# Two blocks of the first expert matrix, and two units of the query weights, joined into one 8 KB piece per partition

## The chip, the cores and the metric

One core of a Trainium2 chip runs the program. The metric is the device time of one execution in microseconds (us), the median of three runs. The engines are PE (TensorE), DVE (VectorE), ACT (ScalarE), POOL (GpSimd) and SP (SyncE); transfers go over the core's 16 DMA engines, which the queues of SP, ACT and POOL share.

## What is computed

Two layers over 256 tokens of width 1024. Each layer has a mixer (attention, a short convolution, gates, projections) and then the PEER block, around which the change lies. Its core, cut from the reference:

```python
q = (hf @ w_query).reshape(T, PEER_HEADS, 2, PEER_HALF)
scores = jnp.einsum("thpd,hpnd->thpn", q, sub_keys)
...
expert_idx = jnp.take_along_axis(cand_i, best_pos, axis=-1)
gates = jax.nn.softmax(best_v, axis=-1)
...
u = jnp.take(expert_u, xc["idx"], axis=0)
vv = jnp.take(expert_v, xc["idx"], axis=0)
a = jax.nn.gelu(jnp.einsum("td,thkd->thk", xc["h"], u))
return jnp.einsum("thk,thkd->td", xc["g"] * a, vv)
```

Each token picks 16 of 16384 experts in each of 8 heads. All matrices are float32; `expert_u` ("U", the first expert matrix) and `expert_v` ("V") have 64 MB each per layer, `w_query` 8 MB.

## The kernel before

**Two ways for two halves of the tokens.** The first 128 tokens are done densely: PE multiplies them by all of U (128 units of 128 experts, `experts`, L1099), a gelu and one-hot weights select what counts (L1071 to L1088), and PE multiplies by all of V (L1157). The other 128 tokens are done by gathers: 256 indirect DMAs per layer, issued by POOL (L991), each bringing one expert row of 4 KB for each of the 128 tokens, half of them from the rows of U and half from the rows of V. DVE takes up each gather: `use` (L1002) multiplies a U row by the token's vector and sums it (L1007), or adds a weighted V row into `y1` (L1015).

**Gathers.** There are eight buffers of 512 KB for them (`NROWS`). `use` hands its buffer back and `issue` (L985) starts the next gather into it, so a gather's time from issue to use cannot be longer than the time in which DVE takes up eight. While the U units run, one `use` stands behind each unit, and beside it a portion of the routing (`route_all`, L1026: top-k and index arithmetic on DVE), until the routing is done. All of this order is fixed when the program is built. `factors` (L897) ends the routing: it turns the selections by PE transposes that DVE copies out, in between its other work.

**The stream of weights.** Everything that is read densely goes through one list, `stream`, in groups of 1 MB: two units of 512 KB in a tile of 128 partitions by 2 by 1024 floats. `pairs` (L79) makes a group of two units that lie one behind the other in memory: the tile's partition then holds 4 KB of one unit and 4 KB of the next. `load_ahead` (L175) walks the list and starts a transfer on SP's queue (L198) whenever a place is free: three `raw` tiles, and, for the query weights and U alone, "spare" places (`spare_part`, L157): parts of the buffers `ah` and `al` that will hold the results later, `hot`, and the gather buffers `rows` before the first gather. So SP has up to 16 places as the query weights end, fewer and fewer during the U stage, and 3 at its end. `dense_done` (L356) gives a place back when PE has issued its matmuls, and SP's transfer waits for these.

For V the two units of a group are neighbours in a row of memory (unit `j` of row `i` is row 128`i`+`j`), so that a partition's 8 KB are one piece already. Ahead of a V group, SP waits for a mark that DVE sets in its own order (`marks`, L195); a U or query group has no such mark. The query weights and U are laid out by `lay_out` on the host (L1220), unit by unit:

```python
"w_query": blocks(np.asarray(i["w_query"]), 16),
"expert_u": np.asarray(i["expert_u"]).reshape(L, 128, 128, KD, 128)
            .transpose(0, 2, 4, 3, 1).reshape(L, 128, 128, D),
```

Of the kernel before, what the change touches and what calls it, by code (L numbers as in the profile page):

```python
# [17 lines left out]
DEPTH, S, D = 2, 256, 1024  # L18
NT = S // 128
KD = D // 128  # L20
# [5 lines left out]
NE = 128  # L26
# [20 lines left out]
def body(ctx: ExitStack, tc: tile.TileContext, d: dict, out: bass.AP):  # L47
    nc = tc.nc
    V, A, G, T = nc.vector, nc.scalar, nc.gpsimd, nc.tensor
# [27 lines left out]
    groups = []  # L77

    def pairs(kind, ap, n):  # L79
        for u in range(0, n, 2):  # L80
            groups.append((kind, [(slice(0, 2), ap[u:u + 2].rearrange("u p c -> p u c"))]))

    def ada_pair(l, r, m):

        a = d["w_adat"]
        return (("col", l, r, m), [(slice(0, 1), a[l, r, m]), (slice(1, 2), a[l, r + 1, m])])

    def ada_rows(l, r, k):
        a = d["w_adag"][l, r].rearrange("(k p) c -> k p c", p=128)
        return (("row", l, r, k), [(slice(0, 2), a[k:k + 2].rearrange("u p c -> p u c"))])  # L90

    def weave(main, extra, first=0):

        extra = deque(extra)
        res, n, m = [], len(extra), len(main) - first
        for i, g in enumerate(main):
            res.append(g)
            while extra and (n - len(extra)) * m < (i + 1 - first) * n:
                res.append(extra.popleft())
        assert not extra  # L100
        return res

    def take_groups():
        g = list(groups)
        groups.clear()
        return g

    stream = []
    for l in range(DEPTH):
        n = NFIRST[l]  # L110
        pairs("qk", d["w_qk"][l, :n], n)
        pairs("v", d["w_v"][l], 4)
        pairs("qk", d["w_qk"][l, n:], 8 - n)
        pairs("conv", d["w_cv"][l], 12)
        pairs("gate", d["w_gt"][l], 16)
        for u in range(4):
            groups.append(("proj", [(slice(0, 1), d["w_ap"][l][u:u + 1].rearrange("u p c -> p u c")),
                                    (slice(1, 2), d["w_cp"][l][u:u + 1].rearrange("u p c -> p u c"))]))
        a = take_groups()
        ex = [ada_rows(l, r, k) for r in range(2) for k in range(0, KD, 2)]  # L120
        if l == 0:
            cols = [ada_pair(0, 0, m) for m in range(KD)]
            parts = {"c": cols, "u": a[:n // 2], "v": a[n // 2:n // 2 + 2]}
            a = a[n // 2 + 2:]
            start = [parts[ch].pop(0) for ch in START]
            assert not any(parts.values())
            ex = [ada_pair(0, 2, m) for m in range(KD)] + ex
        else:
            ex = [ada_pair(l, 2, m) for m in range(KD)] + ex
        pairs("out", d["w_out"][l].rearrange("(k p) c -> k p c", p=128), 8)  # L130
        a += take_groups()
        if l + 1 < DEPTH:
            ex += [ada_pair(l + 1, 0, m) for m in range(KD)]
        if l == 0:
            a = start + weave(a, ex)
        else:
            a = weave(a, ex, 4)
        stream += a
        pairs("query", d["w_query"][l], 16)
        stream += take_groups()  # L140
        u_ap = d["expert_u"][l]
        v_ap = d["expert_v"][l].rearrange("(i j) c -> j i c", j=128)
        for kind, src in (("U", u_ap), ("V", v_ap)):
            for u in range(0, NE, 2):
                groups.append((kind, [(slice(0, 2), src[u:u + 2].rearrange("u p c -> p u c"))]))
        stream += take_groups()

    state = {"dma": 0, "unit": 0, "out": 0, "out0": 0, "v": 0}
# [1040 lines left out]
    for l in range(DEPTH):  # L1189
# [20 lines left out]
        pairs = [xp.tile([128, 2, D], F32, name=f"rows{i}") for i in range(NROWS // 2)]  # L1210
# [9 lines left out]
def lay_out(i):  # L1220
    import numpy as np

    def c(a):
        return np.ascontiguousarray(a)

    L = DEPTH
    w = np.asarray(i["w_in"])
    ada = np.asarray(i["w_ada"]).reshape(L, D, 6, D)
    ab = np.asarray(i["b_ada"]).reshape(L, 6, D)

    def blocks(a, n):
        return a.reshape(L, KD, 128, n, 128).transpose(0, 3, 2, 1, 4).reshape(L, n, 128, D)

    def proj(a):
        a = np.asarray(a).reshape(L, 4, 128, 4, 2, 128).transpose(0, 3, 2, 4, 1, 5)
        return a.reshape(L, 4, 128, D)

    r = {
        "x": np.asarray(i["x"]).reshape(S, D),
        "c": np.asarray(i["c"]),  # L1240
        "c_col": np.asarray(i["c"]).reshape(KD, 128).T,
        "norm_g": np.stack([np.asarray(i["norm1_g"]), np.asarray(i["norm2_g"])], 1).reshape(L, 2, KD, 128).transpose(3, 0, 1, 2),
        "w_adat": ada[:, :, [0, 1, 3, 4]].reshape(L, D, 4, KD, 128).transpose(0, 2, 3, 4, 1),
        "w_adag": ada[:, :, [2, 5]].transpose(0, 2, 1, 3),
        "b_ada": ab[:, [0, 1, 3, 4]].reshape(L, 4, KD, 128).transpose(3, 0, 1, 2),
        "b_gate": ab[:, [2, 5]],
        "w_qk": blocks(w[:, :, :1024], 8).reshape(L, 2, 4, 128, D).transpose(0, 2, 1, 3, 4).reshape(L, 8, 128, D),
        "w_v": w[:, :, 1024:1536].reshape(L, 4, 2, 128, 512).transpose(0, 1, 3, 2, 4).reshape(L, 4, 128, D),
        "w_cv": w[:, :, 1536:3072].reshape(L, KD, 128, 3, 4, 128).transpose(0, 4, 3, 2, 1, 5).reshape(L, 12, 128, D),
        "w_gt": blocks(w[:, :, 3072:], 16),  # L1250
        "conv_w": np.asarray(i["conv_w"]).reshape(L, 3, 4, 128).transpose(3, 0, 2, 1),
        "w_ap": proj(i["w_attn_proj"]),
        "w_cp": proj(i["w_conv_proj"]),
        "w_out": np.asarray(i["w_out"]),
        "w_query": blocks(np.asarray(i["w_query"]), 16),
        "sub_keys": np.asarray(i["sub_keys"]).reshape(L, 16, 128, 128).transpose(0, 3, 1, 2),
        "expert_u": np.asarray(i["expert_u"]).reshape(L, 128, 128, KD, 128).transpose(0, 2, 4, 3, 1).reshape(L, 128, 128, D),
        "expert_v": np.asarray(i["expert_v"]),
        "expert_rows": np.asarray(i["expert_u"]),
        "final_g": np.asarray(i["final_g"]).reshape(1, D),  # L1260
    }
    return {k: c(a) for k, a in r.items()}


def build(arrays):
    import concourse.bacc as bacc

    nc = bacc.Bacc("TRN2", target_bir_lowering=False, num_devices=1)
    d = {}
    for k, a in arrays.items():  # L1270
        d[k] = nc.dram_tensor(f"in_{k}_dram", a.shape, mybir.dt.from_np(a.dtype), kind="ExternalInput").ap()
    o = nc.dram_tensor("out_0_dram", (S, D), F32, kind="ExternalOutput").ap()
    with tile.TileContext(nc) as tc:
        body(tc, d, o)
    return nc
# [9 lines left out]
```

## Time and profile before

| | before |
|---|---|
| time, median of 3 runs | 1833.51 us (1832.49 to 1835.61) |
| the profiled execution | 1834.56 us, its span 1832.8 us |
| PE busy | 1600.5 us (87%) |
| DVE busy | 1390.8 us (76%) |
| POOL, ACT busy | 634.9 us (35%), 577.5 us (32%) |
| moved by DMA | 669.22 MB, mean 365 GB/s |
| chain that ended last | DMA 33%, DVE 31%, PE 26% |

The table is from the profile's page. Shares of busy time are averages over the stages: in each layer the mixer, then the query weights, then U (about 273 to 612 us in the first layer, 1170 to 1505 us in the second), then V. "Chain" is followed back from the last instruction, at each step to what released it.

### The profile page before, as it was taken

Reading aid. Unit: us, or ns where it says so; the run is one execution under the profiler, and the core shown is the slowest. Engines: PE = TensorE matmul, PEld = TensorE weight load, DVE = VectorE, ACT = ScalarE, POOL = GpSimd, SP = SyncE. Lnnn points to the kernel's source line nnn. Section 1 sums busy time; section 2 is a strip of 40 time slices with the busy share of each in tenths; the row PEclk is TensorE's granted clock in tenths of the full one; section 3 lists DMA queues with packets and bytes.
Section 4 is the critical chain, followed back from the end, with each engine's and each line's share of the span. In section 5 each row is a group of like instructions: output and inputs, shape, how many; then the busy total and the mean of one; then the engine's idle time right before and its main releaser. Section 6 shows DMA issues by size and latency. Waiting matters only on the chain.

```text
span 1832.8 us, 26002 instructions
## 1 busy us (share of the span) xinstructions
PE 1600.5 (87%) x9527; PEld 1257.6 (69%) x9527; DVE 1390.8 (76%) x2872; ACT 577.5 (32%) x1257; POOL 634.9 (35%) x540
## 2 busy tenths in 40 slices
PE   6899999968599988977789999997886999888776
PEld 5789779967599645522268997897886994444222
DVE  7798859999888777745467875899997887676455
ACT  3464322111166334200047434221113653331001
POOL 1000004444544555555400000244444445334551
PEclk8899999988899999999999999998898999999999
DMA  8769779999999999999955877899999999999996
GB/s 334 263 228 357 294 312 357 408 408 407 409 368 405 414 414 416 415 415 415 397 218 192 293 278 297 321 391 408 409 404 397 388 403 415 414 415 415 416 414 277
DMA packets 163201, 669.22 MB, mean 365 GB/s; under 512 B 16001, under 2 KB 16001, under 8 KB 146690
## 3 DMA queue, kind: packets, MB, share of 16 engines
q1 hardware_dynamic: 87346, 396.39, 55.1%
q0 software_dynamic: 73856, 268.48, 37.0%
q10 hardware_dynamic: 1872, 2.69, 0.4%
q8 instruction: 75, 1.23, 0.3%
q14 instruction: 52, 0.43, 0.1%
HBM read 666.46 MB, written 1.05 MB: 364 GB/s over the span
## 4 chain that ended last, share of the span: by engine, by line
DMA 33%; DVE 31%; PE 26%; issue 5%; ACT 3%; POOL 1%; SPq 0%; POOLq 0%; DVEq 0%; ACTq 0%
DMA rows<-in_expert_v_dram,idx 20%; DVE rows L1007 8%; PE mm L1099 8%; DMA rows<-in_expert_rows_dram,idx 5%; DMA raw<-in_expert_v_dram 5%; PE yp L1157 4%; PE wp L1086 3%; DVE y L1015 3%; PE mm L394 3%; DVE wl L345 2%; PE mm L395 2%; PE mm L396 2%; DVE raw L288 2%; ACT wh L340 1%; DVE ti L838 1%
## 5 line engine op out<-in xcount | busy, mean ns | idle before, releaser
L991 POOL DMA_INDIRECT rows<-in_expert_rows_dram,idx x256 | 292.2, 1142 | 783.3 <-PE mm L940 239.8
L1015 DVE SCALAR_TENSOR_TENSOR y<-rows,cv,y 128x1024 f32<-128x1024 f32 x254 | 325.7, 1282 | 161.2 <-DMA rows<-in_expert_v_dram,idx 156.4
L991 POOL DMA_INDIRECT rows<-in_expert_v_dram,idx x256 | 327.0, 1277 | 294.4 <-DMA rows<-in_expert_v_dram,idx 105.0
L1007 DVE SCALAR_TENSOR_TENSOR rows<-rows,h 128x1024 f32<-128x1024 f32 x256 | 307.5, 1217 | 19.4 <-DMA rows<-in_expert_rows_dram,idx 19.0
L1157 PE MATMUL yp<-raw,ah 128*128 128x512 f32 x512 | 240.8, 617 | 65.8 <-DMA raw<-in_expert_v_dram 64.6
L1157 PE MATMUL yp<-raw,al 128*128 128x512 f32 x512 | 239.3, 611 | 31.2 <-DMA raw<-in_expert_v_dram 30.3
L1099 PE MATMUL mm<-hfull,raw 128*128 128x128 f32 x1984 | 239.7, 280 | 19.6 <-ACT al L1113 16.8
L1099 PEld LDWEIGHTS mm<-hfull,raw 128*128 128x128 f32 x1984 | 231.1, 195 | 20.4 <-ACT al L1113 17.2
L1071 ACT ACTIVATE hot<-iotf,iT 128x128 f32<-128x128 f32 x512 | 163.4, 390 | 257.8 <-PE wp L1086 212.4
L1157 PEld LDWEIGHTS yp<-raw,ah 128*128 128x128 f32 x512 | 95.3, 194 | 209.8 <-DMA raw<-in_expert_v_dram 108.2
L1099 PE MATMUL mm<-hfull,ah 128*128 128x128 f32 x1600 | 195.1, 284 | 13.3 <-ACT al L1113 13.3
L1099 PEld LDWEIGHTS mm<-hfull,ah 128*128 128x128 f32 x1600 | 191.6, 201 | 13.6 <-ACT al L1113 13.6
L1157 PEld LDWEIGHTS yp<-raw,al 128*128 128x128 f32 x512 | 93.2, 192 | 134.2 <-issue 94.9
L345 DVE TENSOR_TENSOR wl<-raw,wh 128x1024 fp32r<-128x1024 f32 x112 | 135.0, 1222 | 41.4 <-ACT wh L340 40.4
L394 PE MATMUL mm<-hh,wh 128*128 128x256 f32 x512 | 148.5, 290 | 3.8 <-ACT qT L658 3.3
L1086 PEld LDWEIGHTS wp<-hot 128*128 128x128 f32 x1024 | 128.9, 192 | 28.7 <-issue 28.7
L395 PE MATMUL mm<-hl,wh 128*128 128x256 f32 x512 | 145.8, 285 | 0.0
L396 PE MATMUL mm<-hh,wl 128*128 128x256 f32 x512 | 145.7, 285 | 0.0
L340 ACT ACTIVATE wh<-raw 128x1024 fp32r<-128x1024 f32 x112 | 115.8, 1052 | 70.7 <-DMA raw<-in_w_gt_dram 26.6
L1086 PE MATMUL wp<-hot 128*128 128x64 f32 x1024 | 127.8, 268 | 0.0
L394 PEld LDWEIGHTS mm<-hh,wh 128*128 128x128 f32 x512 | 99.2, 194 | 9.9 <-issue 4.0
L395 PEld LDWEIGHTS mm<-hl,wh 128*128 128x128 f32 x512 | 99.2, 194 | 0.0
(228 smaller groups left out, 2112.4 us busy)
## 6 DMA issues: line engine op xcount, KB each, us to landing
raw<-in_expert_v_dram SPq DMA_DIRECT2D x128, 1024.0 KB
raw<-in_expert_u_dram SPq DMA_DIRECT2D x62, 1024.0 KB
ah<-in_expert_u_dram SPq DMA_DIRECT2D x50, 1024.0 KB
raw<-in_w_adat_dram SPq DMA_DIRECT2D x64, 512.0 KB
raw<-in_w_gt_dram SPq DMA_DIRECT2D x16, 1024.0 KB
raw<-in_w_adag_dram SPq DMA_DIRECT2D x16, 1024.0 KB
raw<-in_w_cv_dram SPq DMA_DIRECT2D x12, 1024.0 KB
raw<-in_w_qk_dram SPq DMA_DIRECT2D x8, 1024.0 KB
```

Source lines behind the costliest of these rows:

```text
L340: A.activation(h, raw, AF.Copy)
L345: l_engine().tensor_tensor(lo, raw, f(h), op=OP.subtract)
L394: T.matmul(ps, h[:, c], mh[:, k], start=first, stop=False)
L395: T.matmul(ps, h[:, c], ml[:, k], start=False, stop=False)
L396: T.matmul(ps, lo[:, c], mh[:, k], start=False, stop=last)
L991: G.indirect_dma_start(out=t, out_offset=None, in_=rows[kind], in_offset=bass.IndirectOffsetOnAxis(ap=idx[:, s:s + 1], axis=0))
L1007: V.scalar_tensor_tensor(t, t, 1.0, h1, op0=OP.mult, op1=OP.mult, accum_out=av[:, s:s + 1])
L1015: V.scalar_tensor_tensor(y1, t, cv[:, s:s + 1], y1, op0=OP.mult, op1=OP.add)
L1071: A.activation(p[:, i], iotf, AF.Abs, bias=iT[:, b * TB + i:b * TB + i + 1])
L1086: T.matmul(ps[:, t], p[:, t], q[:, t], start=True, stop=True)
L1099: T.matmul(ps[:, u + x], raw[:, x, k * 128:(k + 1) * 128], hf[:, k, :128], start=(k == 0), stop=(k == KD - 1))
L1157: T.matmul(ys[q], halves[i // 64][:, i % 64], raw[:, x, q * 512:(q + 1) * 512], start=(i == 0), stop=(i == NE - 1))
```

## The change

The host lays two units side by side: for each partition first the 4 KB of the one, then the 4 KB of the other. A new helper `joined` makes one group of each such double unit, so that a partition's 8 KB are one piece in memory. It replaces `pairs` for the query weights (8 groups per layer) and for U (64 groups per layer). V keeps `pairs`, and everything else is as it was: the same 1 MB into the same tiles in the same order.

```diff
+    def joined(kind, ap):
+        for u in range(ap.shape[0]):
+            groups.append((kind, [(slice(0, 2), ap[u])]))
...
-        pairs("query", d["w_query"][l], 16)
+        joined("query", d["w_query"][l])
         stream += take_groups()
-        u_ap = d["expert_u"][l]
-        v_ap = d["expert_v"][l].rearrange("(i j) c -> j i c", j=128)
-        for kind, src in (("U", u_ap), ("V", v_ap)):
-            for u in range(0, NE, 2):
-                groups.append((kind, [(slice(0, 2), src[u:u + 2].rearrange("u p c -> p u c"))]))
+        joined("U", d["expert_u"][l])
+        pairs("V", d["expert_v"][l].rearrange("(i j) c -> j i c", j=128), NE)
         stream += take_groups()
...
+    def two(a):
+        return a.reshape(L, -1, 2, 128, D).transpose(0, 1, 3, 2, 4)
...
-        "w_query": blocks(np.asarray(i["w_query"]), 16),
+        "w_query": two(blocks(np.asarray(i["w_query"]), 16)),
...
-        "expert_u": np.asarray(i["expert_u"]).reshape(L, 128, 128, KD, 128).transpose(0, 2, 4, 3, 1).reshape(L, 128, 128, D),
+        "expert_u": two(np.asarray(i["expert_u"]).reshape(L, 128, 128, KD, 128).transpose(0, 2, 4, 3, 1).reshape(L, 128, 128, D)),
```

SP's transfers at the change from query weights to U in the first layer, before (a name such as `al<-in_expert_u_dram` is place and source, then partitions by pieces by floats):

```order
L198 DMA raw<-in_w_query_dram 128x2x1024 x3
L198 DMA rows_2296<-in_w_query_dram 128x2x1024
L198 DMA al<-in_w_query_dram 128x2x1024 x4
L198 DMA hot<-in_expert_u_dram 128x2x1024
L198 DMA ah<-in_expert_u_dram 128x2x1024 x4
```

The same place in the changed kernel, where L199 is the line that was L198:

```order
L199 DMA raw<-in_w_query_dram 128x2048 x3
L199 DMA rows_2296<-in_w_query_dram 128x2048
L199 DMA al<-in_w_query_dram 128x2048 x4
L199 DMA hot<-in_expert_u_dram 128x2048
L199 DMA ah<-in_expert_u_dram 128x2048 x4
```

Nothing has moved; two pieces of 1024 floats have become one of 2048. The other engines' instructions are the same in the same order. V's transfers have that form before the change already:

```order
L198 DMA raw<-in_expert_v_dram 128x2048 x3
L196 DMA marks<-in_c_dram 1x1
L198 DMA raw<-in_expert_v_dram 128x2048
```

These are SP's first transfers of V in the first layer; the marks stand only there.

## Rows read from the trace of the kernel before

**Rows 1.** Busy time by stretch: us, PE PEld DVE ACT POOL busy (count), clock, DMA share, GB/s

```profile
273.00:487.00 214.00, 187.10 (x1506) 182.70 (x1504) 205.87 (x581) 37.95 (x62) 103.17 (x90) 0.94 1.00 394
487.00:504.00 17.00, 0.17 (x1) 0.17 (x2) 10.90 (x12) 0.19 (x1) 9.80 (x9) 0.57 1.03 410
504.00:612.00 108.00, 108.00 (x943) 108.00 (x944) 88.40 (x173) 65.73 (x171) 49.40 (x44) 0.97 1.00 391
...
1383.00:1398.00 15.00, 0.00 (x0) 0.00 (x0) 9.95 (x9) 0.00 (x0) 8.61 (x8) 0.63 1.03 410
```

**Rows 2.** The same view, saturated stretches of the U and the V stage

```profile
340.00:440.00 100.00, 80.73 (x682) 80.16 (x681) 96.19 (x280) 13.67 (x19) 46.28 (x40) 0.91 1.03 409
...
700.00:900.00 200.00, 164.86 (x463) 76.45 (x463) 117.37 (x194) 29.55 (x75) 110.69 (x83) 0.99 1.02 415
```

**Rows 3.** What DVE waited for, first layer's query and U stage: total us, times, longest

```profile
DVE y L1015 <- DMA rows<-in_expert_v_dram,idx: 6.0, 5, 1.5
...
DVE rows L1007 <- DMA rows<-in_expert_rows_dram,idx: 0.3, 1, 0.3
```

**Rows 4.** The same for the second layer

```profile
DVE y L1015 <- DMA rows<-in_expert_v_dram,idx: 5.0, 5, 1.4
```

**Rows 5.** Groups of DVE's instructions, 300 to 440 us: count, busy, mean ns, idle before

```profile
L1007 DVE SCALAR_TENSOR_TENSOR rows<-rows,h 128x1024 f32<-128x1024 f32 x57 | 68.3, 1214 | 0.3 <-DMA rows<-in_expert_rows_dram,idx 0.3
```

**Rows 6.** The page's DMA packets, and its queues (q1 is SP's, q0 the gathers')

```profile
DMA packets 163201, 669.22 MB, mean 365 GB/s; under 512 B 16001, under 2 KB 16001, under 8 KB 146690
...
q1 hardware_dynamic: 87346, 396.39, 55.1%
```

**Rows 7.** DMA queues (packets, MB, share), U stage, 380 to 400 us

```profile
q0 software_dynamic: 1125, 4.10, 51.6%
q1 hardware_dynamic: 1054, 4.06, 50.8%
```

**Rows 8.** DMA queues, V stage, 852 to 855 us

```profile
q1 hardware_dynamic: 112, 0.92, 73.7%
q0 software_dynamic: 104, 0.37, 30.7%
```

**Rows 9.** SP's timeline in the U stage: start, us, instruction, count

```profile
341.15 0.37 SPq L198 DMA_DIRECT2D al<-in_expert_u_dram  x1
...
348.29 11.09 SPq L198 DMA_DIRECT2D ah<-in_expert_u_dram  x4
362.59 7.51 SPq L198 DMA_DIRECT2D raw<-in_expert_u_dram  x3
388.19 0.37 SPq L198 DMA_DIRECT2D hot<-in_expert_u_dram  x1
391.76 11.09 SPq L198 DMA_DIRECT2D ah<-in_expert_u_dram  x4
```

**Rows 10.** DMA queues and issues, 287 to 373 us

```profile
q1 hardware_dynamic: 4400, 16.99, 50.4%
...
ah<-in_expert_u_dram SPq DMA_DIRECT2D x8, 1024.0 KB
raw<-in_expert_u_dram SPq DMA_DIRECT2D x6, 1024.0 KB
al<-in_expert_u_dram SPq DMA_DIRECT2D x4, 1024.0 KB
hot<-in_expert_u_dram SPq DMA_DIRECT2D x2, 1024.0 KB
```

**Rows 11.** The chain that ended last, 405 to 440 us: start, us, what

```profile
415.52 17.47 DMA rows<-in_expert_rows_dram,idx
```

**Rows 12.** DVE's timeline, 478 to 506 us: start, us, instruction [idle before]

```profile
495.66 1.28 DVE L1015 SCALAR_TENSOR_TENSOR y<-rows,cv,y 128x1024 f32<-128x1024 f32 x1 [1.44 <-DMA rows<-in_expert_v_dram,idx]
498.22 1.28 DVE L1015 SCALAR_TENSOR_TENSOR y<-rows,cv,y 128x1024 f32<-128x1024 f32 x1 [1.28 <-DMA rows<-in_expert_v_dram,idx]
```

**Rows 13.** What PE waited for, 230 to 612 us

```profile
PE wp L901 <- DVE iT L905: 17.1, 1, 17.1
```

## The prediction

> **What bounds the kernel now.** I read the stages first, then who waits in them, then the DMA queues. The change touches only SP's transfers of the query weights and of U, so what counts is what ends last while those are in flight. In the windows [rows 1] the reader should see a U stage of three parts. From 273 to 487 us DVE is busy 205.87 of 214 us: routing and gathers on DVE set the pace, and PE, which could go faster, is tied to it. From 487 to 504 us PE stands still (0.17 us busy) until DVE has copied `iT` out [rows 13], and DVE on its side takes up V gathers as they land. From 504 to 612 us PE is busy all the time. The second layer repeats this; its standstill is from 1383 to 1398 us [rows 1].
>
> The DMA engines are full long before anything waits for them: 409 GB/s with a share of 1.03 from 340 to 440 us [rows 2], where DVE nevertheless waits 0.3 us in all for gathers of U rows [rows 3]. In that stretch DMA is fully used and yet not what ends last. How close it is: the gather issued at 415.52 us took 17.47 us and stands on the chain [rows 11]. DVE takes up 57 gathers in 140 us [rows 5], one per 2.46 us, so eight buffers are one round of 19.7 us; less 1.2 us of use and about 1 us of POOL, some 17.5 us is all that a gather may take. The gathers have **no lead left at 415 us**.
>
> **What the change does to each transfer.** Nothing is added, removed or moved: 64 U and 8 query groups per layer, 1 MB each, in the same places and order. Only the piece changes, from 4 to 8 KB. V's transfers have that form now, so V's rows price it, in two ways.
>
> *The piece itself.* With V in 8 KB pieces the engines move 415 GB/s, with U in 4 KB pieces 409 GB/s [rows 2], 1.5% more. From 334 to 504 us, 170 us of full engines, that would be worth 2.6 us per layer if DMA ended last there. Up to 487 us it does not, DVE does; in the last 17 us it is worth 0.25 us. I take 0. Before 273 us SP runs ahead of PE, after 504 us PE is the bound at 391 GB/s [rows 1]: nothing there either. If that cover were gone, the gain is the 2.6 us.
>
> *The turn.* Beside each other, the gathers' queue and SP's queue move 1125 and 1054 packets from 380 to 400 us, 4.10 and 4.06 MB: half each [rows 7]. Beside V they move 104 and 112 packets, but 0.37 and 0.92 MB [rows 8]. The queues take turns by packet, not by byte, and the 8 KB packet takes twice the turn. So the gathers' share, while U is queued, falls from 4.10 MB in 20 us (205 GB/s, one 0.524 MB gather per 2.56 us) to 0.37 MB in 3 us (123 GB/s, one per 4.26 us). U's share rises to 307 GB/s, one group per 3.42 us. The Trainium skill has such a rule, against this change: by "DMA: Bandwidth & Descriptors", section "Queues, rings and completion order", an engine goes round its queues and switches only at packet boundaries. By it alone, with 9 to 17 descriptors to a packet as the page has it, U would take an even larger share than two thirds; the rows show one piece against one row, and I go by the rows.
>
> DVE wants a gather per 2.46 us. At 2.56 us it was just about served; at 4.26 us it is not. What decides is how long U stays queued. U comes in bursts, as PE frees places: nine groups from 341.15 to 370.10 us, one per 3.57 us, then none until 388.19 us, then six [rows 9]. Now a group needs 3.42 us, so the queue is hardly ever empty during a burst, and empty after it. The worst is the burst of nine, 9 x 3.57 = 32 us. In it 32/4.26 = 7.5 gathers land; DVE wants 32/2.46 = 13.0. It has a lead of landed gathers. With a lead of 5.5 nothing happens; with none DVE stands at its 7.5th gather after 32 us instead of 18.5 us, 13.5 us late. The trace shows a full lead only at the start and none at 415 us [rows 11]; the burst is preceded by some 7 us without U. I take a lead of 3.5, in the middle between none and seven: 11.0 gathers after 32 us instead of 27.1 us, **4.9 us late**. After the burst gathers come faster than DVE works, but DVE is the bound there and does not win the time back. The burst of six, 21.4 us, brings 5.0 gathers against 8.7; a short of 3.7 after 18 us of recess is within the lead, so 0.
>
> A second bound, by bytes: only U that is issued and not landed can overtake. From 287 to 373 us 20 groups were issued (20.97 MB) and 16.99 MB moved [rows 10], so 3.98 MB were waiting, 9.6 us at 415 GB/s. So 0 to 9.6 us for this burst.
>
> *The standstill.* From 487 to 504 us DVE waits 6.0 us in five goes (5.0 us in the second layer) for V gathers that come 2.6 us apart beside the last U groups [rows 3, 4, 12]. If U is through earlier, the gathers get the whole and these waits go: -6.0 us. If U is still queued, five gathers at 4.26 instead of 2.56 us: +8.5 us. The bytes up to 504 us are the same either way. I take 0 and keep both ends.
>
> What is late next: DVE's lateness passes through `iT` [rows 13] to PE, and through PE's full stretch to V's start. V's stage is bound by its own bytes, unchanged. So nothing is absorbed: 2 layers x 4.9 us = +9.8 us. The profiled execution of 1834.56 us becomes 1844.4 us; it stood 1.05 us above the median of 1833.51 us, so **1843.5 us** against that median.
>
> **The rivals.**
> *Faster.* Place: the standstill. Mechanism: U is served sooner, its last groups are through at 487 us, and the V gathers have the engines to themselves; 0.524 MB at 410 GB/s is 1.28 us, as long as one use, so the waits of 6.0 and 5.0 us go [rows 3, 4]. Time: 1833.5 - 11 = 1822.5 us, half of it 1828. It decides if the lead before the burst of nine is 5.5 gathers or more. For it: five waits that are plainly DMA; against it: no lead at 415 us. The Trainium skill is on this side: "Perfetto Trace Analysis", section "DMA Optimizations", counts batching from 2 KB to 4 or 8 KB as the first remedy where a kernel is DMA-bound. The trace agrees by 1.5% only, 409 to 415 GB/s.
> *No change.* The bursts eat the lead and no more, or what is lost in them is won back at the standstill: within 3.7 us of 1833.5 us. For it: 0.3 us of waits now. That the pieces don't become 8 KB belongs here, but is unlikely: of 163201 packets 16511 are not under 8 KB [rows 6], and V alone has 128 groups x 128 partitions = 16384.
> *Much slower.* Each end counts: 9.6 us in the burst and 8.5 us in the standstill, 18.1 us per layer, 36 us at most; the likelier half is 1852 us, beyond that up to 1870 us. It decides if U is still queued when the routing ends.
>
> **How the numbers follow.** Forecast (slower by 4 to 15 us) 0.50, much slower 0.12, no change 0.18, faster 0.20. A measurement of this kernel tells 0.2%, 3.7 us, from no change; so slower 0.62, same 0.18, faster 0.20. The range goes from 1827 us (somewhat beyond half of the faster rival) to 1856 us (somewhat above the likelier half of the much slower one), leaving out about 0.1 on each side. The slower cases' own range is 1838 to 1856 us.
>
> **What would show it.** Right: on the page 163201 - 128 x 128 - 16 x 128 = 144769 packets; in the burst after 340 us some 2.5 times as many bytes on q1 as on q0; DVE waits for gathers of U rows of 3 to 8 us per layer where there were 0.3 us, with gather times up to 20 us on the chain; the standstill later by as much, the PE stretch and the V stage as long as before. Wrong: if the queues show equal bytes, the turn is not by packet; if they show the ratio but DVE's waits stay under 1 us, the lead was larger than 3.5; if the waits appear and the time is the same, they were won back at the standstill, whose 6.0 and 5.0 us would then be shorter.

## The result, and the profile after

The changed kernel takes 1846.41 us (median of 6 runs, 1844.78 to 1850.28) against 1833.27 us for the kernel before beside it: 13.1 us more, a ratio of 1.0066 with a 95% interval of 1.0053 to 1.0079. Slower, as forecast; the forecast time was 1843.5 us. The profiled execution took 1848.49 us, with a span of 1846.7 us.

The piece is what the change says. The page of the changed kernel, packets and SP's queue (packets, MB, share):

```profile
DMA packets 144769, 669.22 MB, mean 362 GB/s; under 512 B 16001, under 2 KB 16001, under 8 KB 109826
...
q1 hardware_dynamic: 68914, 396.39, 54.2%
```

The bytes of [rows 6], in 18432 packets fewer on q1 (87346 to 68914): 64 U and 8 query groups per layer, 128 packets less each.

The stages of the first layer come next. Columns are as in [rows 1]; the stretches are where the changed kernel has its U burst, its standstill and its full PE stretch:

```profile
340.00:440.00 100.00, 75.21 (x630) 74.83 (x629) 87.09 (x250) 15.54 (x21) 41.03 (x37) 0.86 0.98 390
700.00:900.00 200.00, 164.33 (x468) 77.02 (x467) 119.42 (x201) 30.54 (x80) 109.18 (x80) 0.99 1.02 415
...
512.00:619.00 107.00, 106.30 (x939) 106.30 (x940) 88.76 (x175) 65.83 (x171) 49.38 (x44) 0.98 1.01 401
```

From 340 to 440 us DVE was busy 96.19 us before [rows 2] and is 87.09 us now: 9.1 us of DVE have gone, in a stage that DVE bounds. The DMA engines, with longer pieces, moved less there, 390 instead of 409 GB/s: the share fell from 1.03 to 0.98. V's stage (415 GB/s) and PE's full stretch after the standstill (107 us, 108 us in [rows 1]) are as they were.

What DVE waited for, first layer's query and U stage, then the same rows of the second layer:

```profile
DVE rows L1008 <- DMA rows<-in_expert_rows_dram,idx: 9.8, 9, 2.4
DVE y L1016 <- DMA rows<-in_expert_v_dram,idx: 3.0, 2, 2.5
...
DVE rows L1008 <- DMA rows<-in_expert_rows_dram,idx: 8.4, 7, 2.6
DVE y L1016 <- DMA rows<-in_expert_v_dram,idx: 2.7, 2, 2.4
```

Against [rows 3] and [rows 4]: waits for gathers of U rows rise from 0.3 to 9.8 us in the first layer and from none to 8.4 us in the second; the waits at the standstill fall from 6.0 to 3.0 and from 5.0 to 2.7 us. Net +6.5 and +6.1 us, 12.6 us in all, against 13.1 us of the medians.

The place shows in DVE's timeline (start, us, instruction, idle before):

```profile
359.97 1.23 DVE L1008 SCALAR_TENSOR_TENSOR rows<-rows,h 128x1024 f32<-128x1024 f32 x1 [1.19 <-DMA rows<-in_expert_rows_dram,idx]
363.74 1.23 DVE L1008 SCALAR_TENSOR_TENSOR rows<-rows,h 128x1024 f32<-128x1024 f32 x1 [0.82 <-DMA rows<-in_expert_rows_dram,idx]
367.49 1.23 DVE L1008 SCALAR_TENSOR_TENSOR rows<-rows,h 128x1024 f32<-128x1024 f32 x1 [0.80 <-DMA rows<-in_expert_rows_dram,idx]
371.37 1.23 DVE L1008 SCALAR_TENSOR_TENSOR rows<-rows,h 128x1024 f32<-128x1024 f32 x1 [0.93 <-DMA rows<-in_expert_rows_dram,idx]
374.99 1.23 DVE L1008 SCALAR_TENSOR_TENSOR rows<-rows,h 128x1024 f32<-128x1024 f32 x1 [2.38 <-DMA rows<-in_expert_rows_dram,idx]
378.76 1.23 DVE L1008 SCALAR_TENSOR_TENSOR rows<-rows,h 128x1024 f32<-128x1024 f32 x1 [0.82 <-DMA rows<-in_expert_rows_dram,idx]
382.52 1.23 DVE L1008 SCALAR_TENSOR_TENSOR rows<-rows,h 128x1024 f32<-128x1024 f32 x1 [1.82 <-DMA rows<-in_expert_rows_dram,idx]
```

These are all the uses from 360 to 384 us. DVE takes up a gather each 3.76 us (22.55 us for six), not each 2.46 us [rows 5], and waits 8.76 us in seven goes. That is the burst of nine. The queues within it, 350 to 370 us:

```profile
q1 hardware_dynamic: 760, 5.57, 67.4%
q0 software_dynamic: 753, 2.73, 34.0%
```

760 packets against 753, and 5.57 MB against 2.73 MB, where both had 4.1 MB [rows 7]. 2.73 MB in 20 us is one gather of 0.524 MB per 3.84 us: DVE's pace in the burst is the gathers' share. On the chain a gather now stands with 26.91 us from issue to use; before, the only gather of U rows on the chain from 300 to 500 us took 17.47 us [rows 11]:

```profile
325.53 19.30 DMA rows<-in_expert_rows_dram,idx
...
355.59 26.91 DMA rows<-in_expert_rows_dram,idx
```

### The profile page after: what moved, and what is told of

Same layout as the page of the kernel before. It is cut to its first block, busy times and chain, and to the rows that moved or that the text cites. A ratio compares the mean times of both kernels' runs of the same rounds, so it can differ in the third digit from the quotient of the medians.

```text
span 1846.7 us, 25999 instructions
## 1 busy us (share of the span) xinstructions
PE 1594.0 (86%) x9524; PEld 1252.2 (68%) x9527; DVE 1392.4 (75%) x2872; ACT 576.8 (31%) x1257; POOL 638.7 (35%) x540
## 3 DMA queue, kind: packets, MB, share of 16 engines
q1 hardware_dynamic: 68914, 396.39, 54.2%
## 4 chain that ended last, share of the span: by engine, by line
DMA 35%; PE 30%; DVE 27%; issue 4%; ACT 3%; POOL 1%; SPq 0%; DVEq 0%; POOLq 0%; ACTq 0%
DMA rows<-in_expert_v_dram,idx 17%; PE mm L1100 9%; DMA rows<-in_expert_rows_dram,idx 8%; DMA raw<-in_expert_v_dram 6%; DVE rows L1008 6%; PE yp L1158 4%; PE wp L1087 4%; DVE y L1016 3%; PE mm L941 3%; PE mm L395 2%; PE mm L396 2%; PE mm L397 2%; DVE wl L346 2%; DVE raw L289 2%; ACT wh L341 1%
```

## The experiments

The theory: the DMA engines give each queue its turn by packet, an 8 KB packet takes twice as long, so in U's bursts the gathers fall to a third of the bytes and DVE, which bounds the stage, waits. Rivals: the query weights' share of the change, the new layout in memory, a cost of 8 KB pieces wherever they run beside gathers, or mere bandwidth by length of the piece. Ratios are to the kernel before, timed beside each version on the same chip.

**U alone.**

```diff
-        joined("query", d["w_query"][l])
+        pairs("query", d["w_query"][l], 16)
```

(with the old layout of the query weights)

> U in 8 KB pieces, the query weights in 4 KB pieces as before. Theory (turn by packet): the loss is made in the U bursts, so nearly all of it stays: 9 to 13 us above the kernel before, DVE waits for gathers of U rows 7 to 10 us per layer. Rival (the query weights' 8 KB pieces, or what is loaded beside them, cost part of it): no more than 8 us above the kernel before, and the U stage starts at the same time as before instead of 2 us later.

Measured: 1846.21 us, 1.0066 (1.0052 to 1.0080), all of the loss. DVE waits 9.2 us for gathers of U rows in the first layer, and the U stage starts no later than before. It speaks for the theory and against the rival.

**The query weights alone.**

```diff
-        joined("U", d["expert_u"][l])
+        pairs("U", d["expert_u"][l], NE)
```

(with the old layout of U)

> Only the query weights in 8 KB pieces, U as before. Theory: no gather is in flight while the query weights are read, so there is nothing to push back: within 2 us of the kernel before. Rival (the query part costs): 2 to 4 us slower, with PE waiting in the query stage.

Measured: 1833.99 us, 1.0001 (0.9990 to 1.0012): not told from no change. The profile of the changed kernel had shown PE waiting 2.8 us in the first layer's query stage, which looked like a second cost. With this run, and with 2.1 us of the same wait in a kernel whose query weights come as before (nine buffers, 4 KB, below), it goes with the execution and not with the change.

**The new layout, read in 4 KB pieces.**

```diff
-            groups.append((kind, [(slice(0, 2), ap[u])]))
+            groups.append((kind, [(slice(x, x + 1), ap[u][:, x:x + 1]) for x in range(2)]))
```

> The memory layout of the changed kernel, but each group is read by two transfers of 4 KB pieces instead of one of 8 KB. Theory (it is the length of the piece, by the turn of the queues): back to the kernel before, within 4 us; equal bytes of gathers and U in a burst; DVE waits for gathers of U rows under 1 us per layer. Rival (it is the layout, the addresses in memory): as slow as the changed kernel, 11 to 14 us above the kernel before.

Measured: 1836.78 us, 1.0015 (1.0005 to 1.0025). Its queues from 350 to 370 us, in a burst:

```profile
q1 hardware_dynamic: 1114, 4.05, 51.0%
q0 software_dynamic: 1114, 4.06, 50.9%
```

Equal packets, equal bytes, no wait for a gather of U rows in either layer. The addresses are those of the changed kernel and most of the loss is gone: it is the length of the piece. Why 0.15% remains is open; twice as many transfers on SP's queue is one candidate, and the next run (0.02%, with most groups in two transfers) speaks against it.

**8 KB pieces late in the U stage only.**

```diff
-            groups.append((kind, [(slice(0, 2), ap[u])]))
+            if kind == "U" and u >= 44:
+                groups.append((kind, [(slice(0, 2), ap[u])]))
+            else:
+                groups.append((kind, [(slice(x, x + 1), ap[u][:, x:x + 1]) for x in range(2)]))
```

> The layout of the changed kernel; 8 KB pieces only for the last 20 of the 64 U groups of a layer (read while PE is the bound, after the standstill), 4 KB pieces in two transfers for the others and the query weights. Theory: the 8 KB piece hurts only where DVE is the bound and U comes in bursts, so this is within 4 us of the kernel before. Rival (8 KB pieces beside gathers cost everywhere, in proportion): about 20/64 of the loss, 4 us or more above the layout with 4 KB pieces alone.

Measured: 1833.67 us, 1.0002 (0.9992 to 1.0012). 20 of 64 groups have the long piece and cost nothing that can be told. Three of them are issued ahead of the standstill already (474 to 484 us), unlike what was expected; the waits at the standstill stay as they were (6.0 and 5.2 us), and beside the others DVE waits for no gather at all (512 to 612 us in the first layer). The rival of a cost everywhere falls.

**The other way: 2 KB pieces.**

```diff
-        for kind, src in (("U", u_ap), ("V", v_ap)):
...
+        for u in range(NE // 2):
+            groups.append(("U", [(slice(0, 4), u_ap[u].rearrange("h p c -> p h c"))]))
+        pairs("V", v_ap, NE)
```

(from the kernel before: units cut in two in memory, 64 groups of four half units; the query weights as before)

> The other way: U in 2 KB pieces (each unit cut in two in memory), query weights as before. Theory (turn by packet): beside U the gathers now get about two thirds of the bytes, U 2 KB per 4 KB; DVE waits for gathers of U rows stay at 0, and the waits for V gathers at the standstill (6.0 and 5.0 us) fall below 2 us per layer; 3 to 9 us faster than the kernel before, unless U itself comes late for PE. Rival (a longer piece is better and a shorter one worse, for lack of bandwidth): slower than before, by 4 us or more.

Measured: 1852.45 us, 1.0090 (1.0074 to 1.0105), the slowest but one. DVE's waits moved as the theory has it, and the time did not follow: DVE waits for no gather in the first layer's U stage, and 0.4 us for one in the second's. Two of PE's waits are new, here in the first layer:

```profile
PE mm L1102 <- DMA raw<-in_expert_u_dram: 12.7, 11, 2.9
PE mm L1102 <- DMA ah<-in_expert_u_dram: 9.7, 4, 3.8
```

U comes late for PE, 22.4 us of waits in the first layer and 18.2 us in the second, while PE's wait for `iT` shrinks from 17.1 to 0.2 us in the first and from 16.1 to 0.7 us in the second. But the bytes are not what was expected. From 380 to 400 us the gathers move 4.10 MB and U 3.82 MB, nearly the same, and not a third for U. Two neighbouring stretches, 386 to 390 us and 390 to 394 us, show why:

```profile
q1 hardware_dynamic: 562, 1.12, 75.0%
q0 software_dynamic: 124, 0.44, 28.8%
...
q0 software_dynamic: 285, 1.04, 66.4%
q1 hardware_dynamic: 285, 0.57, 36.7%
```

In the second stretch both queues are full: 285 packets against 285, so one piece of 2 KB to one row of 4 KB, and the gathers get two thirds of the bytes. The turn is the expected one. In the first stretch few gathers are there to be moved, and U takes the rest. DVE waits for none of them, so they have landed ahead of it, and with eight buffers no more can be under way than DVE frees: 4.10 MB in 20 us is one gather per 2.56 us, close to DVE's pace of 2.46 us [rows 5]. The gathers cannot use the larger share for long. What remains is that both queues together are slower (7.95 MB in 20 us, 398 GB/s, against 409), and it is U that gets less, 3.82 instead of 4.06 MB [rows 7]. How the 16 us divide is open.

**Pacing U, with 8 KB and with 4 KB pieces.** Two kernels: the changed one and the one before, each with

```diff
-            if kind == "V" and in_step["on"]:
+            if (kind == "V" or (kind == "U" and in_step["u"])) and in_step["on" if kind == "V" else "u"]:
```

where `in_step["u"]` holds from the query stage to the last U group.

> The changed kernel, with the marks of the V stage ahead of the U groups too: SP starts a U group only when DVE has come to its place, so that U comes at DVE's pace (a group per 4.9 us) and not in bursts (one per 3.57 us). Theory (the double turn hurts through bursts): beside paced U the gathers have the engines to themselves for some 30% of the time and are served at about 2.4 us each; DVE waits for gathers of U rows 0 to 3 us per layer, the time within 4 us of the kernel before. Rival (8 KB pieces beside gathers cost whatever their order): 10 us or more above the kernel before.

Measured: 1839.78 us, 1.0027 (1.0016 to 1.0039), 3.4 us above the kernel before by the medians and 5 us by the ratio, at the edge of what was expected and well under the changed kernel. DVE waits for gathers of U rows 0 us in the first layer and 0.6 us in the second: without bursts the 8 KB piece takes nothing from the gathers of U rows that DVE would wait for. What is left goes with another wait: PE now waits for U, 9.5 + 1.5 us in the first layer.

> The kernel before, with the same marks ahead of the U groups: what the pacing does by itself. Theory: in 4 KB pieces the gathers had a little lead left, and the pace gives some more; within 4 us of the kernel before, the waits at the standstill not longer than now. Rival (waiting for DVE makes U late for PE): 4 us or more slower, with PE waiting for U.

Measured: 1845.67 us, 1.0048 (1.0033 to 1.0063). The rival holds: the pacing itself makes U late, and PE waits 9.8 + 4.7 us for it in the first layer. DVE also waits for gathers of U rows, 3.9 us in the first layer and 9.0 us in the second, all behind the standstill. Under the same pacing the long piece is the faster one, and PE's waits for U are shorter with it (11.0 and 10.9 us in the two layers, against 14.5 and 15.5 us). That its larger share of the bytes is the reason fits this, and was not tested by itself.

**Nine buffers, and seven, with 8 KB pieces.** The changed kernel with a ninth buffer from the U stage on (and one less added half way through the V stage), or with one of the eight held back until half way through the V stage:

```diff
-NROWS, MORE = 8, (1, 3)
+NROWS, MORE = 8, (0, 2)
...
+        free.append(xp.tile([128, D], F32, name="rows9"))
```

> The changed kernel with nine gather buffers in the U stage instead of eight (in the V stage as many as before). Theory (what decides is the lead of landed gathers): one more gather of lead, 2.46 us less late per layer and burst that runs out: 3 to 8 us faster than the changed kernel, 1838 to 1843 us. Rival (it is the share of the bytes alone, the lead doesn't matter): as slow as the changed kernel.

Measured: 1835.09 us, 0.9994 (0.9984 to 1.0004): the loss is gone; by the two ratios 0.72% or 13 us less than the changed kernel, more than the 3 to 8 us expected. The waits for gathers of U rows fall to 4.7 and 6.2 us, those at the standstill to 1.1 and 1.3 us; 13.3 us in all, where the changed kernel has 23.9 us.

```diff
+        held = free.pop()
...
+                free.append(held)
```

> The changed kernel with seven gather buffers in the U stage instead of eight, in the V stage as before. Theory: the lead shrinks by one gather, 2.46 us later in each of two bursts and at the standstill; 8 to 18 us slower than the changed kernel. Rival (the share of the bytes alone decides): as slow as the changed kernel, 12 to 14 us above the kernel before.

Measured: 1857.17 us, 1.0108 (1.0092 to 1.0124); by the two ratios 0.42% or 7.7 us above the changed kernel, just under the low end. Not all of it lies in the U stage: the waits for gathers there rise from 23.9 to 29.1 us, and in the first V stage, the first half of which runs with seven buffers too, unlike what was expected, DVE's waits for gathers rise from 66.2 to 77.6 us (620 to 960 us). The shares are the same in all three (350 to 370 us: 760 packets on q1 to 753 on q0 with eight buffers, 768 to 763 with nine, 754 to 756 with seven), so the lead decides: one buffer more is worth 13 us, one less up to 8 us.

**Nine buffers with 4 KB pieces**, as a candidate to beat both:

> The kernel before (4 KB pieces) with nine gather buffers in the U stage instead of eight, in the V stage as many as before. Theory (lead of landed gathers): at half the bytes one more buffer covers most of the standstill's waits (6.0 and 5.4 us) as well; 4 to 10 us faster than the kernel before. Rival (before, the gathers were served well enough and the standstill is bound by bytes): within 3 us of the kernel before.

Measured: 1834.57 us beside 1836.30 us, 0.9991 (0.9982 to 1.0001): not told from no change. The standstill's waits stay for the most part (4.8 and 4.6 us, after 6.0 and 5.0), and the DMA engines move 410 GB/s from 487 to 504 us as before [rows 1], so there the rival is right: the standstill is bound by bytes, and another buffer brings little. No version here beats the kernel before by more than the measurement tells.

## Why the prediction was right, step by step

- **The piece**: right. The packet count is the one foretold, and no stage shows a gain from 8 KB: V's stage and PE's full stretch keep their length.
- **The turn**: right for 8 against 4 KB, 760 to 753 packets, and for 2 against 4 KB where both queues are full, 285 to 285. The rule of the Trainium skill that an engine changes queues only at packet boundaries ("DMA: Bandwidth & Descriptors", section "Queues, rings and completion order") agrees with these counts. The prediction's "even larger share than two thirds" does not follow from it: with as many descriptors to a packet on the one queue as on the other, U would have two thirds as well. The size was off: the ratio in bytes is 2.04 to 1 over 20 us, not 2.5. A gather takes 3.8 us and not 4.26, a U group 3.76 us (5.57 MB in 20 us) and not 3.42. The row it was taken from [rows 8] is no accident of three microseconds, as V shows the same from 857 to 860 us (0.90 and 0.38 MB); why V takes more beside gathers than U does is open. It is a choice, though: over 200 us of the V stage the bytes are equal, 41.99 MB for V and 40.93 MB for the gathers, since V's queue is empty in between (851 to 852 us: 2 packets on q1, 111 on q0). So V's rows held the condition too: the long piece has priority only while it is queued.
- **The burst of nine**: the mechanism and the place were right, and the term too small: 8.8 us in the first layer instead of 4.9. The step that failed is the lead of 3.5 gathers, taken in the middle for lack of a row. Ahead of that burst stand eight groups at the same spacing (SP issues them from 309 to 335 us), which the prediction did not work through, and the changed kernel already waits after them, just before the nine begin at 345.08 us:

```profile
341.07 1.22 DVE L1008 SCALAR_TENSOR_TENSOR rows<-rows,h 128x1024 f32<-128x1024 f32 x1 [0.88 <-DMA rows<-in_expert_rows_dram,idx]
```

  So little of the lead was left. At the measured pace the same formula gives 32 - (32/3.8 + 3.5) x 2.46 = 2.7 us with the lead of 3.5, and 11.3 us with none; the 8.8 us measured correspond to a lead of about one gather.
- **The standstill**: taken as 0, it gave back 3.0 us in the first layer and 2.3 us in the second. Half of the waits went, which fits the faster rival's mechanism (U served sooner, the gathers alone at the end) at half its size.
- **The sum**: +9.8 us forecast, 12.6 us by DVE's waits, 13.1 us measured. Two errors of opposite sign, +3.9 and -3.0 us in the first layer, hide in it, so that the time came so close to 1843.5 us is in part luck.
- **Nothing is absorbed**: right. DVE's lateness passed through `iT` (503.5 us before, 512.4 us now) to PE. Of these 8.9 us, 1.6 us stand ahead of the query stage already (its first product at 244.88 us before, at 246.52 us now), where the kernels here differ by some microseconds from one execution to the next (244.27 us with U alone, 243.28 us with the new layout in 4 KB pieces).
- **The faster rival** and the page "Perfetto Trace Analysis" of the Trainium skill, section "DMA Optimizations", which counts batching small transfers into larger ones as the first remedy where a kernel is bound by DMA: the engines were full here, the pieces twice as long, and the time rose by 0.66%. In the paced pair, where PE waits for U, the long piece wins; that the remedy helps where the stream with the long pieces is the one waited for fits this pair and is not shown beyond it.

Why were the longer pieces not repaid by more bytes? From 340 to 440 us the DMA engines moved 19 GB/s less, 1.9 MB. U ran ahead, and after a burst only the gathers were left: from 386 to 398 us the changed kernel's q1 moves nothing and q0 3.72 MB, 310 GB/s, where the kernel before moved 408 GB/s with both queues. Gathers alone cannot fill the engines for long, as no more than eight can be under way.

## What to carry to other kernels

When two streams share full DMA queues, the length of a piece is also a priority: while both are queued, doubling it for one stream takes bytes from the other. So look first at which stream is waited for, and at the lead of the other. One more buffer was worth 0.72% of the time here; 1.5% more bandwidth (409 to 415 GB/s) shows as a gain in no stage. The lead has to be followed burst by burst, from where it is known to be full. And read shares of bytes from stretches in which both queues are full: a mean over 20 us hid the turn in the run with 2 KB pieces, and one over 200 us hid it in the V stage.

## What the runs showed that was not expected

Shorter pieces for U gave the gathers a priority that they had no use for. One piece went to one row at 2, 4 and 8 KB alike (285 to 285, 1114 to 1114 and 760 to 753 packets), but with 2 KB the gathers were soon all landed, the bytes came out nearly equal, and what the kernel kept was the lower rate, 398 GB/s, and a U that came late. In the V stage, 8 KB pieces took 2.4 to 2.5 times the gathers' bytes where both were queued, in U's burst 2.04 times; the cause of that difference is open.
